# Input projection of a hybrid encoder step: seven products per pair of column tiles for two of three token blocks, with partial sums in scratch

## Chip, cores and metric

The kernel runs on one core of one Trainium2 chip. The metric is device time in microseconds (us) of one execution, the median of the runs shown. One profiled execution gives the trace; its times are counted from the first instruction.

## Reference

One layer of a streaming encoder, for 1024 prompt tokens and 8 x 16 sample tokens, D = 2048, all in float32:

```python
xn = rms_norm(x, norm_g)
u, g_pool, c_q, c_kv, k_r, g_mla = split(xn @ w_in)      # 2048 -> 1024, 1024, 512, 256, 64, 1024
pool_out = multiscale_pool(u) * silu(g_pool)             # windows 2, 4, 8, 16; mean minus token; per-group map
q = rms_norm(c_q) @ w_uq;  ckv = rms_norm(c_kv);  kr = rope(rms_norm(k_r))
attn = block-causal attention over ckv (8 heads) ... ;  mla_out = attn * silu(g_mla)
h = x + concat(pool_out, mla_out) @ w_out
y = h + sigmoid(rms_norm(h) @ w_ple_gate + b) * (p @ w_ple)
```

The change is in the first two lines: the norm, the input projection `xn @ w_in` and, in small part, the pooling.

## The kernel before

**Arithmetic.** A float32 value is held as a high and a low part, both of type float32r. `K.split` (L63) makes them: the high part by a copy on ScalarE (ACT, L68, or L71 with a factor), the low part by a subtraction on VectorE (DVE, L69 or L72). A product (`mm3`, L74) takes three matmuls on TensorE (PE): high x high (L77), low x high (L78), high x low (L79). Each has its own weight load (PEld).

**Tiling.** The 1152 tokens are three blocks of 384 columns (prompt, prompt, 256 prompt plus 128 sample tokens). The contraction of 2048 is 16 row tiles of 128. The input projection has 30 column tiles of 128 plus the rope key of 64 columns, which is held as a high and a low half in one 128-column tile.

**Phase 1** (`phase1`, L131) does the whole input projection. It splits all of x^T times the norm's gain once, into `A0`, `A1`, `A2` (L184, loads L180). It never normalises x: a block's row factors `R` (one over the root mean square) multiply what leaves PSUM. They come from a second reading of x in natural layout, `xnat` (`row_factor`, L191: loads on ACT's queue L196, squares with an accumulator L197, a reciprocal root, a broadcast through three transposes, `spread` L93). Then, for each column tile, `load_w` (L104) brings 4 pieces of weights `wraw` (128x512) over SyncE's queue (SP, L110), splits them into a ring of five `wh`/`wl`, and for each block `project` (L123) runs 16 products, 48 matmuls, into one PSUM bank `mm`:

```python
for i, (kind, ct) in enumerate(cts[9:]):                         # L284, the later column tiles
    w, wn = wn, weights(...)                                     # weights one column tile ahead
    for t in range(NT):
        if kind == "gp":
            gated(pp, kind, ct - 8, t, w)                        # project, times R, SiLU, to scratch
            continue
        ps = mm_bank()
        project(k, ps[:, :TB], w, xh[t], xl[t])
        if late:
            pool.mix(*late)
```

The order of column tiles is: latents and rope key, query latents, pooling gates `gp`, pooling input `u`, attention gates `gm`. The pooling class `Pool` (L375) reads `u` straight from PSUM (L422), forms the window sums by doubling on GpSimd (POOL, L402), the mean minus token on DVE (L406), splits it, and maps it (`mix`, L439: 12 matmuls per output tile, gate L455).

**Hand-over.** Phase 2's first tiles (`load_kv` L561, `latent` L541, keys L597) lie where block 0's `A0` lay, so its loads start when block 0's last product is done, while blocks 1 and 2 of the last column tile still run (`left.close()`, L311).

**Order.** The order of the instructions on each engine is laid down when the kernel is built, by a scheduler that simulates a timeline (`schedule_with_timeline_sim=True`) and prefers what stands earlier in the program. On the chip each engine then runs its list in that order.

Of the kernel before, what the change touches and what calls it, by code (L numbers as in the profile page):

```python
# [14 lines left out]
D = 2048  # L15
# [23 lines left out]
class K:  # L39
    """Shared handles: the context, constants and small helpers."""  # L40
# [22 lines left out]
    def split(self, hi, lo, src, scale=None, eng=None):  # L63
        """src (times a per-partition scale) as hi + lo, each of float32r's width."""
        nc = self.nc
        eng = eng or nc.vector
        if scale is None:
            nc.scalar.activation(hi, src, AF.Copy)  # L68
            eng.tensor_tensor(lo, src, hi, ALU.subtract)  # L69
        else:  # L70
            nc.scalar.activation(hi, src, AF.Copy, scale=scale)  # L71
            eng.scalar_tensor_tensor(lo, src, scale, hi, ALU.mult, ALU.subtract)  # L72
# [8 lines left out]
    def rsqrt(self, pool, y, v, tag):  # L81
        """y = v ** -0.5 for v > 0, by Newton steps from an exponent-halving seed."""
# [10 lines left out]
    def spread(self, pool, ps, out, r):  # L93
        """out[:, j * P + q] = r[q, j] on every partition."""
# [9 lines left out]
def load_w(k, wp, src, chunks=range(KT // WKC), scales=None, bufs=5):  # L104
    """Row chunks of a column tile of a weight [128, KT, 128], as hi and lo tiles of WKC row tiles."""
# [17 lines left out]
def project(k, ps, w, xh, xl, kts=range(KT)):  # L123
    """psum[128, TB] = w^T x over the row tiles kts, of which x holds just these."""
# [5 lines left out]

def phase1(k, sc):  # L131
# [5 lines left out]
    es, left = ExitStack(), ExitStack()  # L137
    # the first block's input leaves before the others'
    ap = [left.enter_context(tc.tile_pool(name="p1a", bufs=1, reuse_waits="tile")),
          es.enter_context(tc.tile_pool(name="p1b", bufs=1, side="right", reuse_waits="tile"))]  # L140
    wp = es.enter_context(tc.tile_pool(name="p1w", bufs=1, side="right", reuse_waits="tile"))
    rp = es.enter_context(tc.tile_pool(name="p1r", bufs=1, side="right", reuse_waits="tile"))
    mp = es.enter_context(tc.tile_pool(name="p1m", bufs=1, space=PSUM, reuse_waits="tile"))
    xh, xl = zip(*[[k.t(ap[t > 0], [P, KT, TB], f"A{t}{x}", F32R) for x in "hl"] for t in range(NT)])
    R = [k.t(rp, [P, TB], f"R{t}") for t in range(NT)]

    def mm_bank():
        return k.t(mp, [P, 512], "mm", bufs=4)

    def aux_bank():  # L150
        return k.t(mp, [P, 512], "aux", bufs=2)

    # order of the column tiles: latents and rope key first, gates of B last
    cts = [("ckv", 20), ("ckv", 21), ("kr", 0)] + [("cq", 16 + i) for i in range(4)]
    cts += [("gp", 8 + i) for i in range(8)] + [("u", i) for i in range(8)]

    def weights(kind, ct):
        if kind != "kr":
            return load_w(k, wp, io["w_in"][ct])
        out = []  # L160
        for c in range(KT // WKC):
            raw = k.t(wp, [P, WKC, DR], "wraw", bufs=3)
            nc.sync.dma_start(raw[:], io["w_kr"][:, c * WKC:(c + 1) * WKC, :])
            hl = k.t(wp, [P, WKC, P], "wh", F32R, bufs=5)
            k.split(hl[:, :, :DR], hl[:, :, DR:], raw[:])
            out.append(hl)
        return out
# [6 lines left out]
    w0 = {}  # L174
    with tc.tile_pool(name="p1x", bufs=1, side="right", reuse_waits="tile") as xp:
        for t in range(NT):
            # the very first pieces are short
            for a, b in ([(0, 1), (1, 2)] if t == 0 else [(0, 2)]) + [(j, j + 2) for j in range(2, KT, 2)]:
                raw = k.t(xp, [P, 2, TB], "xraw", bufs=8)
                nc.sync.dma_start(raw[:, :b - a, :], io["xT"][t][:, a:b, :])  # L180
                if t == 0 and a % WKC == 0:
                    w0.update(load_w(k, wp, io["w_in"][cts[0][1]], [a // WKC]))
                if t == 0 and a == 0:
                    consts(k)  # L184
                for i in range(a, b):
                    k.split(xh[t][:, i, :], xl[t][:, i, :], raw[:, i - a, :], k.norm_g[:, i:i + 1])

    nc.sync.dma_start(k.ident[:], io["ident"])
    stats = [(k.t(rp, [P, 3, 4], f"part{t}"), k.t(rp, [P, 3], f"ssq{t}"), k.t(rp, [P, 3], f"inv{t}")) for t in range(NT)]

    def row_factor(xp, t, j):  # L191
        """Sums of squares of token tile j of block t; after the last one the block's row factors, in steps."""
        part, v, r = stats[t]
        for i in range(4):
            raw = k.t(xp, [P, D // 4], "xnat", bufs=3)
            nc.scalar.dma_start(raw[:], io["xN"][3 * t + j][:, i * D // 4:(i + 1) * D // 4])  # L196
            nc.scalar.activation(raw[:], raw[:], AF.Square, accum_out=part[:, j, i:i + 1])  # L197
        if j == 2:
            nc.vector.tensor_reduce(v[:], part[:], AX.X, ALU.add)
            nc.vector.tensor_scalar(v[:], v[:], 1.0 / D, EPS, ALU.mult, ALU.add)  # L200
            k.rsqrt(xp, r[:], v[:], "rs")
            yield
            yield
            yield
            k.spread(xp, aux_bank(), R[t], r)

    def latent_factor(lp, kind, t, acc):
        """The row factors of a block's latents, from the lanes' sums of squares."""
        yield
        yield  # L210
        a = aux_bank()
        for j in range(3):
            nc.tensor.matmul(a[:, j:j + 1], acc[:, j * P:(j + 1) * P], k.ones[:, :1], start=True, stop=True)
        r = stats[t][2]
        v = k.t(lp, [P, 3], "lv")
        s = k.t(lp, [P, 3], "ls")
        nc.vector.tensor_tensor(v[:], r[:], r[:], ALU.mult)
        nc.vector.scalar_tensor_tensor(v[:], a[:, :3], 1.0 / (KVR if kind == "ckv" else QR), v[:], ALU.mult, ALU.mult)
        nc.vector.tensor_scalar_add(v[:], v[:], EPS)
        k.rsqrt(lp, s[:], v[:], "lrs")  # L220
        nc.vector.tensor_tensor(s[:], s[:], r[:], ALU.mult)
        yield
        yield
        out = k.t(lp, [P, TB], "srow")
        k.spread(lp, aux_bank(), out, s)
        nc.sync.dma_start(sc["s_" + kind][t][:], out[:])

    def gated(pool, kind, n, t, w):
        ps = mm_bank()
        project(k, ps[:, :TB], w, xh[t], xl[t])  # L230
        k.tick()
        ev = k.t(pool, [P, TB], "ev", bufs=3)
        nc.vector.tensor_tensor(ev[:], ps[:, :TB], R[t][:], ALU.mult)  # L233
        nc.scalar.activation(ev[:], ev[:], AF.Silu)
        nc.sync.dma_start(sc[kind][t][:, n, :], ev[:])

    # latents: raw projections and their row factors, normalised where they are read back
    with tc.tile_pool(name="p1c", bufs=1, side="right", reuse_waits="tile") as lp:
        kc = k.t(lp, [P, 9, DR], "kc")
        ks = k.t(lp, [P, 9, DR], "ks")  # L240
        rope_tables(k, lp, kc, ks, io["k_rope_g2"], 1.0)
        acc = {}
        for i, (kind, ct) in enumerate(cts[:7]):
            w, wn = (w0 if i == 0 else wn), weights(*cts[i + 1])
            for t in range(NT):
                ps = mm_bank()
                if kind == "kr":
                    for kt in range(KT):
                        st = w[kt // WKC][:, kt % WKC, :]
                        nc.tensor.matmul(ps[:, :TB], st, xh[t][:, kt, :], start=kt == 0, stop=False)  # L250
                        nc.tensor.matmul(ps[:, :TB], st, xl[t][:, kt, :], start=False, stop=kt == KT - 1)
                    k.tick()
                    k.later(rope_key(k, lp, aux_bank, ps, R[t], kc, ks, t, sc))
                    continue
# [25 lines left out]
    with tc.tile_pool(name="p1p", bufs=1, side="right", reuse_waits="tile") as pp:  # L280
# [20 lines left out]
        for t in range(NT):  # L301
            gated(pp, "gm", 0, t, w)
            if t == 0:
                pool.mix(*late)
# [1076 lines left out]
```

## Time and profile before

| | |
|---|---|
| runs (us) | 2322.14, 2326.36, 2325.97; median 2325.97 |
| span of the profiled execution | 2321.7 us; its own time is not listed apart, the nearest run is 0.4 us above the span, the median 4.3 us |
| phase 1 on PE | first matmul at 5.9 us, last of block 2 at 826.7 us |
| PE busy over the span | 2263.2 us (97%) |
| DVE, ACT, POOL busy | 1153.4, 844.8, 382.3 us |
| mean granted TensorE clock | 0.990 |

Busy PE is not PE at its peak: the records of neighbouring matmuls overlap (a 128x384 matmul is recorded with some 335 ns, and one starts every 173 ns or so). Work on PE is therefore read from counts and starts, and idle PE from the waits. What an engine other than PE does costs time only where PE ends up waiting for it.

### The profile page before, as it was taken

Reading aid. Unit: us, or ns where it says so; the run is one execution under the profiler, and the core shown is the slowest. Engines: PE = TensorE matmul, PEld = TensorE weight load, DVE = VectorE, ACT = ScalarE, POOL = GpSimd, SP = SyncE. Lnnn points to the kernel's source line nnn. Section 1 sums busy time; section 2 is a strip of 40 time slices with the busy share of each in tenths; the row PEclk is TensorE's granted clock in tenths of the full one; section 3 lists DMA queues with packets and bytes.
Section 4 is the critical chain, followed back from the end, with each engine's and each line's share of the span. In section 5 each row is a group of like instructions: output and inputs, shape, how many; then the busy total and the mean of one; then the engine's idle time right before and its main releaser. Section 6 shows DMA issues by size and latency. Waiting matters only on the chain.

```text
span 2321.7 us, 35417 instructions
## 1 busy us (share of the span) xinstructions
PE 2263.2 (97%) x13198; PEld 2207.8 (95%) x13198; DVE 1153.4 (50%) x2636; ACT 844.8 (36%) x1967; POOL 382.3 (16%) x357
## 2 busy tenths in 40 slices
PE   8899999999999999989999799999999999999999
PEld 8899999999999989978898699999999999999998
DVE  6443111334312169868988865555553335344343
ACT  6421111111111166766665453434342234222222
POOL 0000000123300000014443342212002221111110
PEclk9999999999999999999999899999999999999999
DMA  7522212333312186573221663434263334223221
GB/s 279 171 98 69 74 65 82 70 88 92 81 61 75 47 244 185 152 221 104 83 68 54 217 204 126 152 128 150 88 190 100 110 106 130 85 86 101 85 86 63
DMA packets 219661, 271.05 MB, mean 117 GB/s; under 512 B 38112, under 2 KB 160480, under 8 KB 219488
## 3 DMA queue, kind: packets, MB, share of 16 engines
q1 hardware_dynamic: 199616, 242.43, 33.4%
q10 hardware_dynamic: 19872, 26.35, 3.4%
q8 instruction: 104, 1.70, 0.3%
q14 instruction: 69, 0.57, 0.1%
HBM read 196.10 MB, written 72.61 MB: 116 GB/s over the span
## 4 chain that ended last, share of the span: by engine, by line
PE 80%; DVE 8%; DMA 7%; issue 2%; ACT 1%; POOL 1%; SPq 0%; ACTq 0%; DVEq 0%; POOLq 0%
PE mm L79 18%; PE mm L77 18%; PE mm L78 18%; PE f L77 3%; PE f L79 3%; PE f L78 3%; DMA xnat<-xN 2%; PE k L78 2%; PE k L77 2%; PE k L79 2%; PE t L919 1%; PE pb L77 1%; PE pb L79 1%; PE o L79 1%; PE pb L78 1%
## 5 line engine op out<-in xcount | busy, mean ns | idle before, releaser
L77 PE MATMUL mm<-A0h,wh 128*128 128x384 f32 x736 | 250.3, 340 | 6.7 <-ACT A0h L71 5.9
L78 PE MATMUL mm<-A0h,wl 128*128 128x384 f32 x736 | 249.7, 339 | 1.0 <-DVE wl L69 1.0
L79 PE MATMUL mm<-A0l,wh 128*128 128x384 f32 x736 | 249.8, 339 | 0.0
L77 PE MATMUL mm<-A1h,wh 128*128 128x384 f32 x736 | 246.6, 335 | 0.2 <-ACT ev L263 0.2
L79 PE MATMUL mm<-A2l,wh 128*128 128x384 f32 x736 | 246.6, 335 | 0.0
L77 PE MATMUL mm<-A2h,wh 128*128 128x384 f32 x736 | 246.5, 335 | 0.0
L78 PE MATMUL mm<-A2h,wl 128*128 128x384 f32 x736 | 246.4, 335 | 0.0
L79 PE MATMUL mm<-A1l,wh 128*128 128x384 f32 x736 | 246.3, 335 | 0.1
L78 PE MATMUL mm<-A1h,wl 128*128 128x384 f32 x736 | 246.3, 335 | 0.0
L69 DVE TENSOR_TENSOR wl<-wraw,wh 128x512 fp32r<-128x512 f32 (+1 forms) x232 | 157.4, 679 | 153.4 <-ACT wh L68 147.7
L68 ACT ACTIVATE wh<-wraw 128x512 fp32r<-128x512 f32 (+1 forms) x236 | 137.4, 584 | 246.8 <-PE mm L79 193.6
L77 PEld LDWEIGHTS mm<-A0h,wh 128*128 128x128 f32 x736 | 139.3, 189 | 7.4 <-ACT A0h L71 5.9
L78 PEld LDWEIGHTS mm<-A0h,wl 128*128 128x128 f32 x736 | 139.2, 189 | 1.8 <-DVE wl L69 1.8
L79 PEld LDWEIGHTS mm<-A0l,wh 128*128 128x128 f32 x736 | 139.1, 189 | 0.2 <-DVE A0l L72 0.2
L79 PEld LDWEIGHTS mm<-A1l,wh 128*128 128x128 f32 x736 | 138.2, 188 | 1.0 <-DVE A1l L72 0.7
L77 PEld LDWEIGHTS mm<-A1h,wh 128*128 128x128 f32 x736 | 138.2, 188 | 0.8 <-ACT ev L263 0.5
L77 PEld LDWEIGHTS mm<-A2h,wh 128*128 128x128 f32 x736 | 138.2, 188 | 0.0
L79 PEld LDWEIGHTS mm<-A2l,wh 128*128 128x128 f32 x736 | 138.2, 188 | 0.0
L78 PEld LDWEIGHTS mm<-A2h,wl 128*128 128x128 f32 x736 | 138.2, 188 | 0.0
L78 PEld LDWEIGHTS mm<-A1h,wl 128*128 128x128 f32 x736 | 138.2, 188 | 0.0
L233 DVE TENSOR_TENSOR ev<-mm,R 128x384 f32<-128x384 f32 x48 | 26.8, 558 | 224.3 <-PE mm L79 224.3
L1239 DVE TENSOR_TENSOR ev<-mm,R 128x384 f32<-128x384 f32 x48 | 26.8, 557 | 174.1 <-PE mm L79 170.2
(437 smaller groups left out, 5511.6 us busy)
## 6 DMA issues: line engine op xcount, KB each, us to landing
wraw<-w_in SPq DMA_DIRECT2D x120, 256.0 KB, 3.1
wraw<-w_out SPq DMA_DIRECT2D x64, 256.0 KB, 3.6
wraw<-w_ple_gate SPq DMA_DIRECT2D x64, 256.0 KB, 3.3
xnat<-xN ACTq DMA_DIRECT2D x36, 256.0 KB, 3.5
ple<-ev ACTq DMA_DIRECT2D x48, 192.0 KB, 2.5
fev<-xT SPq DMA_DIRECT2D x48, 192.0 KB, 2.4
hp<-fev SPq DMA_DIRECT2D x48, 192.0 KB, 1.9
ev<-hp SPq DMA_DIRECT2D x48, 192.0 KB, 2.3
```

The source lines that it names most:

```text
L68: nc.scalar.activation(hi, src, AF.Copy)
L69: eng.tensor_tensor(lo, src, hi, ALU.subtract)
L77: mm(out, sh, mh, start=start, stop=False)
L78: mm(out, sl, mh, start=False, stop=False)
L79: self.last = mm(out, sh, ml, start=False, stop=stop)
L233: nc.vector.tensor_tensor(ev[:], ps[:, :TB], R[t][:], ALU.mult)
L919: nc.tensor.transpose(tp[:, x, :], e[:, (c + x) * P:(c + x + 1) * P], k.ident[:])
L1239: nc.vector.tensor_tensor(g[:], ps[:, :TB], R[t][:], ALU.mult)
```

## The change

For blocks 0 and 1, the two token blocks together with the two halves of a contraction chunk make a 2 x 2 block matrix, and a pair of column tiles with the same halves make another. Their product is formed by Strassen's scheme in Winograd's form: seven products instead of eight, from sums of the input blocks (`S1` to `S4`) and sums of the weight tiles. Because the sums need normalised inputs, x of blocks 0 and 1 is normalised before it is split. The contraction is cut into two chunks of 8 row tiles. The order becomes:

1. *Front.* Chunk 0 of block 2 alone, plain, for the first 26 column tiles (24 matmuls each), while x of blocks 0 and 1 is loaded, its squares are summed, and the operands of chunk 0 are formed.
2. *Chunk 0*, 15 pairs: seven products of 4 row tiles (84 matmuls), block 2 only in the last two pairs. Results go to scratch (`part1`). Meanwhile the operands of chunk 1 are formed and put in scratch (`sums`) in pairs 5, 7, 9 and 11.
3. *Switch.* The 28 operands of chunk 1 come back from scratch and are split; block 2's next 8 row tiles too.
4. *Chunk 1*, 15 pairs: 84 matmuls plus 48 for block 2. The chunk-0 sums are read back and either copied into a PSUM bank before the product (by ACT) or added after it (by DVE). The pooling now reads `u` back from scratch, and its window sums move from GpSimd to DVE.
5. *Hand-over.* Phase 2's loads start after the last pair; block 2 of the last two column tiles (48 matmuls) follows.

The `xnat` loads are gone. Weights are split in pieces of 8 row tiles (128x1024), again in a ring of five; the raw pieces have three buffers. The last two products of a pair (`tail`) are issued after the next pair's first two. The rope key keeps its four products per chunk. Core of the diff:

```diff
+    def sums(self, src, c, rest):                       # weights of a pair, one pair ahead
+        r0, r1 = [self.raw(s, c) for s in src]
+        w0 = self.hl(r0)
+        a = k.t(self.tp, [P, 8, P], "wt")
+        sub(a[:, :4], r1[:, :4], r0[:, :4], ALU.subtract)
+        sub(a[:, 4:], r1[:, 4:], a[:, :4], ALU.subtract)
+        w12 = self.hl(a)
+        sub(r0[:, :4], r1[:, 4:], r1[:, :4], ALU.subtract)
+        sub(r0[:, 4:], r0[:, 4:], a[:, 4:], ALU.subtract)
+        w34 = self.hl(r0)
+        w1 = self.hl(r1, 0 if rest else 4)
+        return {1: (w0, 0), 2: (w0, 4), 5: (w12, 0), 6: (w12, 4), 7: (w34, 0), 4: (w34, 4), 3: (w1, 4),
+                "rest": ((w0, 0), (w1, 0))}
...
+    def pair(self, c0, c1, A, X, W, prior, done, between):
+        def bank(*i):
+            ps = self.bank()[:, :TB]
+            if prior and i:
+                nc.scalar.activation(ps, prior(*i)[:], AF.Copy)
+            return ps
...
+        a, b = bank(), bank(c0, 1)
+        q = prior and prior(c0, 0)
+        self.product(a, x("11"), W[1], True)
+        s1 = tile("s1", 2)
+        nc.scalar.activation(s1[:], a, AF.Copy)
+        d = bank(c1, 1)
+        self.product(b, x("S2"), W[6], start)
+        u2 = tile("u2", 2)
+        add(u2[:], b, s1[:], ALU.add)
+        self.tail()                                     # W[4], W[3] of the pair before
+        between(0)
+        e = [X and bank(c0, 2)]
+        self.product(a, x("12"), W[2], False)
+        done(c0, 0, a, q)
+        self.product(d, x("S1"), W[5], start)
+        between(1)
+        e.append(X and bank(c1, 2))
+        self.product(b, x("S3"), W[7], False)
+        u3 = tile("u3")
+        add(u3[:], b, s1[:], ALU.add)
...                                                     # with X: both tiles of block 2, 24 matmuls each
+    steps += [lambda c=c: row(c) for c in range(16)] + [norms, normalise]
+    steps += [lambda j=j: first_operands(j) for j in range(4)]
+    for i in range(EARLY):                              # front; EARLY = 26
+        w, wn = wn, qk.hl(qk.raw(src[i + 1], 0)) if i + 1 < EARLY else None
+        e = bank()[:, :TB]
+        qk.product(e, X, (w, 0), True, 8)
+        step(2)
+        keep(i, 2, e, None)
...
+    def row(c):                                         # one row tile of blocks 0 and 1: 768 columns
+        for t in range(2):
+            nc.scalar.dma_start(raw[:, t * TB:(t + 1) * TB], io["xT"][t][:, c, :])
+        squares(R, raw[:], ...)                         # ACT square, DVE add
+    def operands(j, a11, a12, a21, a22, s, put):        # 7 splits, 4 subtractions
...
+    for n in OPS:                                       # switch: "11", "S2", "12", "S1", "S3", "22", "S4"
+        for j in range(4):
+            raw = k.t(ap, [P, TB], f"a{j}")
+            nc.sync.dma_start(raw[:], sc["sums"][:, 4 * OPS.index(n) + j, :])
+            put(n, j, raw[:])
...
-            nc.gpsimd.tensor_tensor(nxt[..., a:L], cur[..., a:L], cur[..., a - step:L - step], ALU.add)
+            nc.vector.tensor_tensor(nxt[..., a:L], cur[..., a:L], cur[..., a - step:L - step], ALU.add)
...
-        nc.vector.tensor_tensor(u[:, HIST:], ps[:, :n], R[:, :n], ALU.mult)
+        nc.sync.dma_start(u[:, HIST:], src[t][:, ct, :])
...
+    left.close()                                        # after the last pair's tail
+    yield
+    for i in range(2):                                  # block 2 of the last two column tiles
+        e = bank()[:, :TB]
+        nc.scalar.activation(e, prior(2 * last + i, 2)[:], AF.Copy)
+        qk.product(e, X, W["rest"][i], False, 8)
```

More of the change, by code (lines that the diff above doesn't have):

```diff
@@ L157, in weights @@
[L157 to L167, printed above, removed]
+    xp = es.enter_context(tc.tile_pool(name="p1x", bufs=1, side="right", reuse_waits="tile"))
@@ L171, in phase1 @@
     nc.scalar.activation(k.ones[:], k.ones[:], AF.Copy)
[L174 to L186, printed above, removed]
@@ L188, in phase1 @@
-    nc.sync.dma_start(k.ident[:], io["ident"])
[L189 to L205, printed above, removed]
@@ new lines, in last_block, with squares @@
+    def last_block(c, j):
+        i = 8 * c + j
+        raw = (o_tile() if c else k.t(rp, [P, 2 * TB], f"x{j}"))[:, :TB]
+        nc.sync.dma_start(raw, io["xT"][2][:, i, :])
+        hl = [k.t(xp, [P, TB], f"X{j}{x}", F32R) for x in "hl"]
+        k.split(hl[0][:], hl[1][:], raw, k.norm_g[:, i:i + 1])
+        if c == 0:
+            squares(R2, raw, raw)
+        return hl
+    begun = set()
+    def squares(acc, raw, sq):
+        if id(acc) not in begun:
+            begun.add(id(acc))
+            nc.scalar.activation(acc[:], raw, AF.Square)
+        else:
+            nc.scalar.activation(sq, raw, AF.Square)
+            nc.vector.tensor_tensor(acc[:], acc[:], sq, ALU.add)
@@ new lines, in factors @@
+    def factors(pool, acc, n, dim, wait=1):
+        a = aux_bank()
+        for j in range(n):
+            nc.tensor.matmul(a[:, j:j + 1], acc[:, j * P:(j + 1) * P], k.ones[:, :1], start=True, stop=True)
+        v = k.t(pool, [P, n], f"fv{n}")
+        r = k.t(pool, [P, n], f"fr{n}")
+        nc.vector.tensor_scalar(v[:], a[:, :n], 1.0 / dim, EPS, ALU.mult, ALU.add)
+        k.rsqrt(pool, r[:], v[:], f"frs{n}")
+        for _ in range(wait):
+            yield
+        for j in range(0, n, 3):
+            k.spread(pool, aux_bank(), acc[:, j * P:(j + 3) * P], r[:, j:j + 3])
@@ new lines, in phase1, with chunk, weights @@
+    OPS = ("11", "S2", "12", "S1", "S3", "22", "S4")
+    pairs = range(KR // 2)
+    def chunk(c, prior, done, between, pairs=pairs):
+        def weights(m):
+            return qk.sums(src[2 * m:2 * m + 2], c, c or 2 * m >= EARLY)
+        W = weights(pairs[0])
+        for m in pairs:
+            if m == 2:
+                key(c, prior, done)
+            Wn = weights(m + 1) if m + 1 in pairs else None
+            qk.pair(2 * m, 2 * m + 1, A, X if c or 2 * m >= EARLY else None, W, prior, done, lambda i: between(m, i))
+            W = Wn
@@ new lines, in prepare @@
+    def prepare(m, i):
+        if i == 1 and m in (5, 7, 9, 11):
+            second_operands((m - 5) // 2)
+        if i == 1 and m < 4:
+            square_rest(8 + 2 * m)
+            square_rest(9 + 2 * m)
+        if i == 1 and m == 4:
+            k.later(factors(ep, R2, 3, D))
+        if i == 0:
+            k.tick()
+    chunk(0, None, keep, prepare)
+    qk.tail()
+    for n in OPS:
[3 more added lines that the diff above has]
+            put(n, j, raw[:])
@@ new lines, in phase1, with mixer @@
+    pool = Pool(k, mp, aux_bank, inv, sc, wp)
+    def mixer(m, i):
+        if 8 <= m < 12 and i == 0:
+            g = m - 8
+            for t in range(NT):
+                steps.extend([lambda c=c, t=t: pool.tile(2 * g + c, t) for c in range(2)])
+                if t:
+                    steps.append(lambda t=t: pool.mix(g, t - 1))
+                else:
+                    steps.append(lambda: pool.weights(g))
+                steps.append(pool.split)
+            steps.append(lambda: pool.mix(g, NT - 1))
+        step(2)
@@ L313, in phase1 @@
+    chunk(1, prior, finish, mixer, range(6, KR // 2 - 1))
+    last = KR // 2 - 1
+    W = qk.sums(src[2 * last:], 1, True)
+    qk.pair(2 * last, 2 * last + 1, A, None, W, prior, finish, lambda i: mixer(last, i))
+    qk.tail()
+    left.close()
+    yield
+    for i in range(2):
+        e = bank()[:, :TB]
+        nc.scalar.activation(e, prior(2 * last + i, 2)[:], AF.Copy)
+        qk.product(e, X, W["rest"][i], False, 8)
+        finish(2 * last + i, 2, e, None)
+        step(len(steps))
     es.close()
```

388 lines of the change are left out of this document (252 added, 136 removed).

## Prediction

> **What bounds the kernel now.** I read the page's head first, then the busy time by stages, the groups of matmuls, and the waits of PE up to the end of phase 1. Columns of a stage: its length, then busy time of PE, PEld, DVE, ACT and POOL with counts, granted clock, DMA share, GB/s. A wait row ends with total, times, longest.
>
> ```profile
> span 2321.7 us, 35417 instructions
> PE 2263.2 (97%) x13198; PEld 2207.8 (95%) x13198; DVE 1153.4 (50%) x2636; ACT 844.8 (36%) x1967; POOL 382.3 (16%) x357
> ...
> 6.00:100.00 94.00, 84.57 (x448) 80.42 (x449) 50.04 (x122) 59.92 (x141) 0.00 (x0) 0.96 0.75 259
> 100.00:826.00 726.00, 726.00 (x4190) 725.65 (x4189) 208.13 (x463) 124.06 (x216) 66.18 (x104) 1.00 0.26 78
> ...
> 200.00:400.00 200.00, 200.00 (x1157) 199.89 (x1156) 41.33 (x92) 34.42 (x59) 0.11 (x1) 1.00 0.21 69
> ...
> L77 PE MATMUL mm<-A0h,wh x480: 335/338/688, 5.9 to 809.7; 128*128 128x384 f32 x160
> L79 PE MATMUL mm<-A2l,wh x480: 334/334/421, 30.8 to 826.7; 128*128 128x384 f32 x160
> ...
> PE mm L77 <- ACT A0h L71: 5.9, 1, 5.9
> PE aux L100 <- DVE sq L98: 4.5, 2, 2.4
> PE aux L213 <- ACT R L101: 2.9, 1, 2.9
> ```
>
> PE bounds it. From 100 to 826 us it never idles; one matmul starts every 200 / 1157 = 0.173 us at full clock, with DVE busy 29% and ACT 17%. The only losses of phase 1 stand in its first 100 us: the start, and the chain of the row factors. So each matmul taken out of phase 1 is worth 0.173 us, as long as DVE, ACT and the queues, which have room, stay ahead.
>
> **The matmuls.** Before: 30 column tiles x 3 blocks x 48 = 4320, plus 96 for the rope key. After: front 26 x 24 = 624; two chunks x 15 pairs x 7 products x 12 = 2520; block 2 in the pairs, 4 x 24 + 30 x 24 = 816; rope key again 96. Together 4056, which is 360 fewer: **-62.3 us**. The mixer's 144 matmuls and the transposes stay. Everything else in the change can only take from this, except the front.
>
> Prices (mean ns in the grouped rows; the rows that begin with a time have start and us):
>
> ```profile
> L69 DVE TENSOR_TENSOR wl<-wraw,wh 128x512 fp32r<-128x512 f32 x26 | 18.0, 693 | 34.5 <-ACT wh L68 34.4
> L69 DVE TENSOR_TENSOR wql<-raw,wqh 128x768 fp32r<-128x768 f32 x8 | 7.6, 953 | 1.6 <-ACT wqh L68 1.6
> 816.12 1.23 DVE L69 TENSOR_TENSOR wkl<-raw,wkh 128x1024 fp32r<-128x1024 f32 x1
> L233 DVE TENSOR_TENSOR ev<-mm,R 128x384 f32<-128x384 f32 x19 | 10.6, 558 | 100.5 <-PE mm L79 100.5
> L69 DVE TENSOR_TENSOR dl<-d,dh 128x384 fp32r<-128x384 f32 x24 | 13.8, 573 | 11.3 <-ACT dh L68 11.3
> L72 DVE SCALAR_TENSOR_TENSOR A0l<-xraw,gains,A0h 128x384 fp32r<-128x384 f32 x16 | 8.9, 617 | 0.8 <-ACT A0h L71 0.8
> L455 DVE SCALAR_TENSOR_TENSOR ev<-aux,gains,ev 128x384 f32<-128x384 f32 x24 | 14.4, 611 | 5.9 <-PE aux L79 4.4 <-DMA ev<-gp 1.5
> L406 DVE SCALAR_TENSOR_TENSOR d<-s,u 128x384 f32<-128x384 f32 x16 | 8.9, 555 | 13.5 <-POOL s L402 13.5
> L68 ACT ACTIVATE ch<-raw 128x1024 fp32r<-128x1024 f32 x16 | 16.9, 1055 | 18.4 <-PE k L79 11.7 <-DMA raw<-cache_T 6.7
> L263 ACT ACTIVATE ev<-mm 128x384 f32<-128x384 f32 x18 | 8.4, 487 | 36.4 <-PE mm L79 36.4
> ev<-gp SPq DMA_DIRECT2D x24, 192.0 KB, 2.4
> ```
>
> **Chunk 0, 15 pairs of 84 matmuls, 14.5 us each.** DVE has 4 subtractions (4 x 0.69), splits of 3.5 pieces (3 x 1.23 + 0.69) and 7 operations on 384 columns (7 x 0.56): 11.1 us. ACT has 3.7 splits and copies, about 5 us. In pairs 5, 7, 9 and 11 the operands of chunk 1 add 4 x 0.62 + 4 x 0.56 = 4.7 us, so 15.8 of 14.5. The ring of five allows this delay: the slot of the next pair's first weights comes free after `W[3]` of the pair before, that of its second after `W[2]`; each is wanted three products (6.2 us) later, and copy plus subtraction take 1.06 + 1.23. So 3.9 us of lateness on DVE is free in each pair. How PE fares beside a full DVE is seen in later stages of this kernel:
>
> ```profile
> 850.00:900.00 50.00, 49.72 (x291) 47.52 (x290) 42.20 (x132) 37.24 (x138) 0.00 (x0) 0.98 0.59 178
> 1100.00:1150.00 50.00, 48.31 (x295) 45.53 (x294) 44.56 (x87) 32.31 (x64) 21.87 (x15) 1.00 0.21 69
> 1200.00:1250.00 50.00, 46.72 (x289) 43.83 (x288) 45.38 (x87) 31.03 (x62) 22.96 (x14) 1.00 0.15 54
> 1250.00:1300.00 50.00, 44.47 (x240) 39.38 (x238) 43.57 (x99) 24.74 (x52) 16.78 (x12) 0.93 0.35 107
> 1300.00:1350.00 50.00, 41.83 (x227) 37.27 (x228) 40.77 (x78) 29.40 (x69) 24.74 (x21) 0.86 0.79 251
> ```
>
> With DVE at 84% PE loses 0.6%, with DVE at 91% 6.6%. On the 243 us of chunk 0 that is 1 to 16 us; DVE averages (15 x 11.1 + 4 x 4.7 + 5) / 243 = 78% there, nearer the first: **+2**.
>
> **Chunk 1, 15 pairs of 132 matmuls, 22.8 us.** DVE: 2.8 + 4 x 1.23 + 9 x 0.56 = 12.7 us; room enough in pairs 0 to 7. From pair 8 the pooling comes on top, all on DVE now: window sums by L406's price, 20 doublings x (3 x 0.555 or so, the third block in two pieces), 35; the means 14; splits 24 x 0.573 = 14; gates 24 x 0.611 = 15: some 80 us. Pairs 8 to 14 take PE 7 x 22.8 + 144 x 0.173 = 185 us, DVE 7 x 12.7 + 80 = 169, or 91%. By the two rows above 1 to 12 us: **+5**. The seeding of PSUM (4 per pair) waits for a load and an ACT copy, 2.4 + 0.49; six banks let it start two products (4.1 us) ahead, so I cost it at nothing; without this cover it is 2.9 us per pair, 44 in all. SP issues some 14 transfers per pair. A weight load behind one that waits for DVE waits too; that is in the 5.
>
> **Switch.** 28 operands and 8 tiles of block 2 (192 KB each) and 1 MB of weights, 8 MB, against the 27 us of pair 14: 300 GB/s; DVE 28 x 0.573 + 8 x 0.62 + 7.7 = 29 us in the same time. Operands leave in the order in which PE last uses them, so most of it can run under pair 14. The nearest row is 1300 to 1350, a change of stage at 251 GB/s: PE idle 8.2 us, and 0.14 of the clock besides (7 us). Bounds 0 and 15, **+5**.
>
> **Front.** The first matmul still waits for one split each of x and weights (5.9). Then per column tile (24 matmuls, 4.15 us) 512 KB of weights come in and 192 KB go out; the row tiles add 6 MB: 27 MB in 114 us, 233 GB/s, less than the 259 that the first 100 us carry now. DMA volume is no new bound, but the engines are tight:
>
> ```profile
> 0.00:25.00 25.00, 17.22 (x81) 15.03 (x82) 18.12 (x34) 19.64 (x36) 0.20 (x4) 1.00 0.92 335
> ...
> ACT xnat L197 <- DMA xnat<-xN: 26.9, 22, 4.5
> ...
> 48.29 0.33 ACTq L196 DMA_DIRECT2D xnat<-xN  x1
> ...
> 93.27 0.83 PE L213 MATMUL aux<-ones,acc 128*128 128x1 f32 x6 [2.87 <-ACT R L101]
> ...
> 95.00:96.70 1.70, 1.70 (x7) 1.70 (x6) 1.43 (x9) 0.18 (x1) 0.00 (x0) 0.50 0.96 340
> ```
>
> ACT stood 26.9 us waiting for 36 loads of x. The new loop has 16 row tiles of the same kind: 26.9 x 16 / 36 = 12 us of such waits. Beside them ACT has, per column tile, 1.06 + 2 squares of 768 columns (0.85 each, between the rows of 384 and 1024) + 0.49 + the issue of four loads (0.33 each): 4.6 against 4.15 us, 4 us over 8 column tiles. After the last of them DVE has a block of work that ranks before later weights: normalising 8 x 0.95, operands 28 x 0.573 + 16 x 0.56, 33 us. The five slots feed PE for 5 x 4.15 = 21 us, so up to 12 us are lost. Upper bound 12 + 4 + 12 = +28. The gain side: the waits for the row factors (4.5 + 2.9) and the slow clock after them go away, since nothing needs them until the operands: -10. In between, **+8**.
>
> [...]
>
> **Hand-over.** Rows of before:
>
> ```profile
> 810.10 0.34 PE L79 MATMUL mm<-A0l,wh 128*128 128x384 f32 x1
> 810.47 0.56 SPq L538 DMA_DIRECT2D raw<-w_kv  x1
> 826.30 1.23 DVE L69 TENSOR_TENSOR wvl<-raw,wvh 128x1024 fp32r<-128x1024 f32 x1 [1.45 <-ACT wvh L68]
> ```
>
> Phase 2's first four weight pieces take 17 us from the release, and 96 matmuls (16.6 us) covered that. Now 48 matmuls (8.3 us) stand there, so up to 8.7 us show. But the released memory is 28 separate operands, of which several end one to six products before the tail; **+2**.
>
> **Sum.** -62.3 + 2 + 5 + 5 + 8 + 2 = -40 us. The profiled span of 2321.7 becomes 2281.5; it lies 4.3 us under the median 2325.97, so the forecast against the median is **2286 us**.
>
> **Rivals.**
> - *Everything is hidden*: only the matmuls count, 2326 - 62 = 2264, down to 2254 with the front's gain. For it: phase 1 shows no PE wait after 100 us. Against: DVE doubles its load there.
> - *The front starves*: +28 instead of +8, 2306. For it the 26.9 us row.
> - *Slower: the weight ring in both chunks.* If the low part of the next weights stands behind a whole set of sums and one output (7.2 + 1.1 us) in DVE's list, a chunk-0 pair lasts 4.4 us more, 15 x 4.4 = 66: 2352. It decides against the change from 2.7 us per pair, a lateness of 6.6. For it: the sums of the next pair stand ahead of this pair's outputs in the program; against: the row 850 to 900.
> - *The clock oscillates.* Three banks are cycled every 12 matmuls instead of one every 48; short waits at each change could bring the 0.93 of the row 1250 to 1300 over all of phase 1's 730 us: 2286 + 51 = 2337. No wait at a change of bank shows between 100 and 826 us. [...]
> - *No gain*: matmuls in the new order start 0.010 us later each (40 / 4056), 2326. No row speaks for it.
>
> **Chances.** Forecast 0.53 (own range 2270 to 2302), all hidden 0.15, front 0.12, ring 0.13, clock 0.04, no gain 0.03. Low end between the hidden case's two values, 2256; high end 2330, which leaves out ring and clock above and little below. What a measurement can tell is about 0.2% (4.6 us): faster 0.79, same 0.04, slower 0.17.
>
> **What would show it.** 4056 `mm` matmuls in phase 1 at 0.173 us; its last about 40 us earlier; PE waits for DVE low parts in the front after some 50 us, few in chunk 0; DVE near 75% in chunk 0, 90% in the pooling pairs; a dip of PE and 250 GB/s or more near 360 to 390 us. The forecast falls if PE waits for `w` low parts in every pair, or if the front runs past 140 us.

## Result and the profile after

The changed kernel took 2343.03 us (median; 2336.01 to 2347.59) where the kernel before took 2326.16: ratio 1.0070, 95% interval 1.0052 to 1.0088. Timed again later beside three of its variants it took 2332.44 us against 2323.72, ratio 1.0036 (1.0023 to 1.0048); a single execution in between took 2322.7. It is slower, by 0.4 to 0.7% in the two sittings (sets of runs timed together) with more than one execution, where 1.7% faster was forecast.

Two profiles are used: the first (2347.59 us, span 2345.8), the longest of its four executions, and that of the second timing (2327.80 us, span 2326.0), the shortest of its five. Head of the page of the first:

```profile
span 2345.8 us, 35907 instructions
PE 2232.0 (95%) x12856; PEld 2168.6 (92%) x12856; DVE 1472.4 (63%) x3096; ACT 975.2 (42%) x2117; POOL 316.4 (13%) x261
```

PE is busy 31 us less than before and idle 55 us more. Where, the windows show; I cut them at front, chunk 0, pairs 0 to 7 of chunk 1, pairs 8 to 14 (the pooling), hand-over (to phase 2's first key product), rest. Columns as in the prediction. The first profile, then the second:

```profile
0.00:129.00 129.00, 117.12 (x643) 113.84 (x644) 91.94 (x135) 76.07 (x122) 0.20 (x4) 0.97 0.70 228
129.00:386.80 257.80, 251.11 (x1415) 250.43 (x1414) 187.47 (x295) 88.30 (x129) 0.00 (x0) 0.98 0.53 166
386.80:590.70 203.90, 199.38 (x1154) 197.80 (x1153) 139.70 (x310) 86.44 (x147) 0.22 (x2) 0.99 0.55 170
590.70:829.70 239.00, 206.39 (x1093) 203.26 (x1091) 152.38 (x298) 63.82 (x108) 0.67 (x6) 0.91 0.61 159
829.70:1043.20 213.50, 190.56 (x1050) 171.42 (x1049) 164.37 (x500) 139.52 (x467) 1.94 (x8) 0.98 0.62 188
1043.20:2345.80 1302.60, 1267.41 (x7509) 1231.81 (x7509) 736.58 (x1559) 521.07 (x1145) 313.37 (x241) 0.98 0.37 117
```
```profile
0.00:127.20 127.20, 116.93 (x642) 113.96 (x643) 91.80 (x135) 76.56 (x122) 0.20 (x4) 0.97 0.69 231
127.20:383.60 256.40, 249.95 (x1415) 249.27 (x1414) 188.31 (x296) 89.73 (x131) 0.00 (x0) 0.99 0.52 168
383.60:586.90 203.30, 199.29 (x1155) 197.89 (x1154) 138.10 (x309) 85.16 (x145) 0.22 (x2) 0.99 0.53 168
586.90:816.30 229.40, 201.34 (x1093) 197.53 (x1091) 153.03 (x299) 64.23 (x109) 0.67 (x6) 0.95 0.62 166
816.30:1029.40 213.10, 192.89 (x1051) 174.13 (x1049) 164.27 (x501) 140.07 (x467) 1.95 (x8) 0.96 0.62 190
1029.40:2326.00 1296.60, 1263.53 (x7509) 1227.78 (x7509) 735.12 (x1559) 521.09 (x1145) 313.27 (x241) 0.99 0.36 117
```

The same cuts of the kernel before: its first 100 us and its end from the last projection product:

```profile
0.00:100.00 100.00, 84.65 (x448) 80.50 (x449) 50.81 (x123) 62.78 (x145) 0.20 (x4) 0.97 0.74 256
826.70:1025.60 198.90, 188.40 (x1052) 173.32 (x1050) 158.81 (x492) 135.61 (x461) 2.28 (x8) 0.97 0.62 186
1025.60:2321.70 1296.10, 1263.47 (x7509) 1227.62 (x7509) 735.21 (x1559) 522.04 (x1145) 313.68 (x241) 0.99 0.37 117
```

Length less count times 0.173 is what a stage loses (counts of a window may miss or gain a few records; I use the program's: 642, 1413, 1152 and 1091 with the mixer's products and transposes):

| term | forecast | first profile | second |
|---|---|---|---|
| 360 matmuls fewer | -62.3 | -62.3 | -62.3 |
| front, against 22.4 lost before | +8 | -4 | -6 |
| chunk 0 | +2 | +13 | +12 |
| switch and pairs 0 to 7 | +5 | +5 | +4 |
| pairs 8 to 14 with the pooling | +5 | +50 | +41 |
| hand-over, against 198.9 | +2 | +15 | +14 |
| rest, against 1296.1 | 0 | +7 | +1 |
| sum | -40 | +24 | +4 |

The spans differ from before by +24.1 and +4.3. One term carries most of the error, 45 of the 64 us in the first profile: the pooling pairs. Of their 50 us some 33 are idle time of PE (239.0 less 206.4), and nearly all the rest is the granted clock of 0.91 in that row (206.4 x 0.09 = 19 us, an estimate). There, in the first profile (waits of PE, DVE and SP's queue in 590 to 830 us; total, times, longest):

```profile
PE aux L77 <- DVE ev L726: 25.5, 6, 11.0
PE aux L77 <- ACT dh L68: 5.5, 2, 5.0
```
```profile
DVE s L675 <- DMA u<-u: 32.7, 16, 6.3
DVE ev L726 <- DMA ev<-gp: 22.2, 13, 5.3
```
```profile
SPq L721 <- DMA mixp<-ev: 29.4, 17, 6.3
SPq L727 <- DVE ev L726: 21.4, 14, 4.8
```

PE waits 25.5 us for the gated product (`ev`, L726), because its two auxiliary banks are both still unread. DVE is not full there (152.4 of 239 us, 64%): it stands waiting for what comes back from scratch, `u` (L675) and the gate (L726). And SP's queue, which issues nearly everything, waits 29.4 us to issue the next gate load (L721) until the store of the last product from the same single buffer has landed. A stretch of 31 us from the chain of waits of that profile, start and us, has it in line:

```profile
736.57 5.64 DMA mixp<-ev
742.23 4.25 DMA ev<-gp
746.58 0.62 DVE ev L726
747.22 1.85 DMA mixp<-ev
749.09 2.53 DMA ev<-gp
751.85 0.44 issue
752.39 5.09 DMA mixp<-ev
757.55 2.63 DMA ev<-gp
760.20 0.63 DVE ev L726
760.84 1.88 DMA mixp<-ev
762.78 4.53 DMA ev<-gp
```

Store, load, 0.6 us of work, store, load: in this stretch PE and ACT are off the chain, and DVE is on it for 0.6 us at a time. Later in the stage (768 to 802 us) the chain also holds runs of DVE's own operations, beside loads of `u`.

### The profile page after: what moved, and what is told of

Same layout as the page of the kernel before. It is cut to its first block, busy times and chain, and to the rows that moved or that the text cites. A ratio compares the mean times of both kernels' runs of the same rounds, so it can differ in the third digit from the quotient of the medians.

```text
span 2345.8 us, 35907 instructions
## 1 busy us (share of the span) xinstructions
PE 2232.0 (95%) x12856; PEld 2168.6 (92%) x12856; DVE 1472.4 (63%) x3096; ACT 975.2 (42%) x2117; POOL 316.4 (13%) x261
## 4 chain that ended last, share of the span: by engine, by line
PE 50%; DVE 8%; DMA 8%; issue 2%; ACT 1%; POOL 0%; SPq 0%; ACTq 0%; DVEq 0%; POOLq 0%
PE mm L77 8%; PE mm L79 8%; PE mm L78 8%; PE f L77 3%; PE f L79 3%; PE f L78 3%; PE k L79 2%; PE k L78 2%; PE k L77 2%; PE t L1190 1%; DMA ev<-gp 1%; PE pb L77 1%; PE s L78 1%; PE s L77 1%; PE pb L79 1%
## 5 line engine op out<-in xcount | busy, mean ns | idle before, releaser
L68 ACT ACTIVATE wh<-wraw 128x1024 fp32r<-128x1024 f32 (+3 forms) x233 | 178.7, 769 | 233.3 <-PE mm L177 141.9
L69 DVE TENSOR_TENSOR wl<-wraw,wh 128x1024 fp32r<-128x1024 f32 (+3 forms) x231 | 205.8, 892 | 64.8 <-ACT wh L68 61.8
L1511 ACT ACTIVATE ev<-ev,gains 128x384 f32<-128x384 f32 x48 | 29.4, 612 | 224.5 <-DVE ev L1510 124.4
L77 PE MATMUL k<-wkh,ch 128*128 128x448 f32 x256 | 96.3, 377 | 2.5 <-ACT ch L68 1.4
L1318 DVE TENSOR_REDUCE v<-sq 128x8 f32<-128x1024 f32 x64 | 77.7, 1213 | 14.5 <-ACT sq L1317 14.2
L79 PE MATMUL mm<-A2l,wh 128*128 128x384 f32 x256 | 86.1, 336 | 0.0
L77 PE MATMUL mm<-A2h,wh 128*128 128x384 f32 x256 | 86.0, 336 | 0.0
L77 PE MATMUL mm<-A0h,wh 128*128 128x384 f32 x256 | 85.8, 335 | 0.0
L79 PE MATMUL mm<-A0l,wh 128*128 128x384 f32 x256 | 85.7, 335 | 0.0
L78 PE MATMUL mm<-A1h,wl 128*128 128x384 f32 x256 | 85.7, 335 | 0.0
L78 PE MATMUL mm<-A0h,wl 128*128 128x384 f32 x256 | 85.7, 335 | 0.0
L79 PE MATMUL mm<-A1l,wh 128*128 128x384 f32 x256 | 85.5, 334 | 0.0
L77 PE MATMUL mm<-A1h,wh 128*128 128x384 f32 x256 | 85.5, 334 | 0.0
```

Source lines behind the costliest of these rows:

```text
L77: mm(out, sh, mh, start=start, stop=False)
L78: mm(out, sl, mh, start=False, stop=False)
L79: self.last = mm(out, sh, ml, start=False, stop=stop)
L1318: nc.vector.tensor_reduce(v[:, j, :], sq[:].rearrange("p (h d) -> p h d", h=H), AX.X, ALU.add)
L1511: nc.scalar.activation(g[:], g[:], AF.Sigmoid, bias=k.b_ple_gate[:, ct:ct + 1])
```

## Experiments

All ratios are to the kernel before, timed beside it, with 95% intervals.

**First set: one suspect each.** Two gate buffers; two input buffers; window sums back on GpSimd; no gate.

```diff
-            gate = k.t(pp, [P, TB], "ev")                     # e1_gate2
+            gate = k.t(pp, [P, TB], "ev", bufs=2)
-        u = k.t(pp, [P, HIST + TB], "u")                      # e6_u2
+        u = k.t(pp, [P, HIST + TB], "u", bufs=2)
-            nc.vector.tensor_tensor(nxt[..., a:L], ...)       # e2_gpsimd
+            nc.gpsimd.tensor_tensor(nxt[..., a:L], ...)
-            nc.sync.dma_start(gate[:], sc["gp"][t][:, n, :])  # e4_nogate; the product is scaled per channel only
```

> The changed kernel with two buffers instead of one for the mixer's gate tile. Theory A (the gate's one buffer makes store, next load and scaling a chain of some 5 us per output, DVE stands in line for the load, PE for the PSUM bank): PE's waits for the scaling from 615 to 826 us fall from 25.5 us to under 10, most of the half-clock time after them goes too, 20 to 35 us faster than the changed kernel's median of 2343. Theory B (DVE is simply full in the pooling pairs, because the window sums moved to it): within 5 us of 2343, and the waits stay.

> The changed kernel with two buffers instead of one for the pooling input tile that is read back from scratch. Theory A in its narrow form (the gate's buffer alone): within 5 us of 2343. Theory A in its wide form (every load from scratch into a single buffer stands in DVE's line; DVE idled 33 us before the first window sum): DVE's idle time before the window sums falls from 33 to under 15 us and the time by 8 to 20 us. Theory B: within 5 us.

> The changed kernel with the window sums back on GpSimd, all else as changed. Theory A: no gain, within 8 us of 2343 to either side, since a sum lasts 0.85 us on GpSimd against 0.57 on DVE and the chain gets longer. Theory B (DVE's load): DVE loses some 35 us of work between 615 and 826 us, PE's waits there halve, 15 to 25 us faster.

> The changed kernel with the mixer's gate left out: the mapped output is scaled by the per-channel scale alone and stored, and the gate is never loaded. Theory A: the load is gone from the chain, only the store of 2 us stands between two scalings; the waits for the scaling nearly vanish and it is 25 to 40 us faster than 2343, a little more than with two buffers. Theory B: at most 5 us, since DVE's work is the same.

| | time (us) | ratio | pairs 8 to 14 (us) |
|---|---|---|---|
| two gate buffers | 2324.51 | 0.9998 (0.9984 to 1.0012) | 220.1 |
| two input buffers | 2333.2 | 1.0035 (1.0022 to 1.0047) | 223.2 |
| sums on GpSimd | 2338.74 | 1.0072 (1.0052 to 1.0091) | 233.5 |
| no gate | 2326.7 | 1.0008 (0.9998 to 1.0018) | 216.6 |

Taking the window sums off DVE gained nothing, though not on equal terms, since DVE then waited 22.7 us for GpSimd's sums. It points away from DVE's amount of work as the bound; the run without loads, below, decides it. The other three shorten the stage. Without the gate PE still waited 12.9 us for the scaled product, and 16 us were gained in the reading below where 25 to 40 were expected: the gate's load is not the whole loss. I read 18.5 and 10 us of gain for the buffers against the first timing of the changed kernel, made in another sitting; that reading did not hold (below).

**Second set: the edits together, and the other two terms.** Both buffers; the second half's operands held on DVE to the pairs they were written for; the last two block-2 tiles held behind the tail; all four.

```diff
+        k.mark = add(u2[:], b, s1[:], ALU.add).ins            # e8_held
-            second_operands((m - 5) // 2)
+            with tc.issue_after(k.mark):
+                second_operands((m - 5) // 2)
     qk.tail()
+    held = k.last.ins                                         # e3_tailfirst
...
+        with tc.issue_after(held):
+            qk.product(e, X, W["rest"][i], False, 8)
```

> Gate tile and pooling input tile both with two buffers (the small window tile of the last tile of each channel borrows a slot of the output ring to make room). Theory A (single buffers chain the loads, each its own chain): the gains add, 2343 - 18.5 - 10 = 2314; 2311 to 2319, last product of phase 1 at 800 to 805 us, PE's waits for the gate product and DVE's waits for the pooling input both under 10 us between 590 and 830. Rival (one chain, and either buffer already breaks it): no more than the better of the two, 2322 to 2326, last product near 809.

> Only the second half's operands are held on DVE behind the pair they are written for (pairs 5, 7, 9 and 11 of the first chunk). Theory C (the loss of chunk 0 is these operands, issued at 135 to 185 us with the key's weights and the squares): PE's window 150 to 175 goes from 18.3 to over 23 us at a clock over 0.9, chunk 0 shortens by 8 to 12 us, time 2331 to 2336. Rival D (chunk 0 has no room for the operands anywhere; a later pair loses what this one gains): chunk 0 stays within 3 us, time 2340 to 2345.

> Only the two block-2 tiles held back for the hand-over are issued behind the last pair's tail, so all 48 of their matmuls cover it instead of 24. Theory E (the cover of the hand-over was half spent early): PE's waits from 826 to 900 us fall from 13.8 to 8 to 10, last product of phase 1 to first key product from 213.5 to 208 to 210, time 2337 to 2341. Rival F (the fill in the pooling stage was worth as much as the cover, or the waits are loads that 4 us of cover do not reach): time 2342 to 2346.

> All four edits: two buffers for gate and pooling input, second operands held to their pairs, block-2 tiles behind the tail. If the three losses are separate, the sum is 2343 - 28 - 10 - 4 = 2301, and 2296 to 2308, faster than the kernel before by about 1 per cent. If they share one cause (DVE's total work, so that what one place gains another gives back) it stays at 2316 to 2326, no faster than the kernel before or hardly.

| | time (us) | ratio | chunk 0 | pairs 8 to 14 | hand-over |
|---|---|---|---|---|---|
| both buffers | 2320.69 | 0.9993 (0.9981 to 1.0004) | 256.4 | 222.7 | 209.0 |
| operands held | 2325.0 | 1.0008 (0.9999 to 1.0017) | 251.2 | 229.2 | 213.0 |
| tiles behind tail | 2332.94 | 1.0041 (1.0025 to 1.0056) | 257.0 | 232.5 | 208.7 |
| all four | 2311.41 | 0.9943 (0.9930 to 0.9955) | 251.2 | 221.7 | 210.9 |

The buffers do not add: 222.7 us with both, 220.1 and 223.2 with one. That is the rival's number, but one chain is not shown by it: to make room, this edit also puts the pooling's small state tile into the ring of the outputs, and DVE waits there for an output store (`gm<-o`, 7.4 us) as with neither single edit. All four together, 2311.4 us, lie between the two forecasts (2296 to 2308 if the losses are separate, 2316 to 2326 if they are one). What still waits with both buffers is seen in the all-four profile's waits of SP's queue in 590 to 826 us: the same line, now L725, still 32.4 us.

```profile
SPq L725 <- DMA mixp<-ev: 32.4, 11, 4.6
SPq L532 <- ACT o L531: 18.5, 9, 7.9
```

The cause in chunk 0 is shown in size only for part of it: the window 150 to 175 of the changed kernel, then of the one with held operands, and DVE's operations on those operands in 130 to 190 us of the first (12 of 16 normalisations, written for pairs 5 to 11, 219 to 322 us):

```profile
150.00:175.00 25.00, 18.31 (x78) 17.67 (x77) 20.07 (x36) 6.07 (x9) 0.00 (x0) 0.80 0.91 291
```
```profile
150.00:175.00 25.00, 22.63 (x128) 21.88 (x127) 14.75 (x23) 8.67 (x13) 0.00 (x0) 1.00 0.46 157
```
```profile
L463 DVE SCALAR_TENSOR_TENSOR a<-a,gains,R 128x384 f32<-128x384 f32 x12 | 7.3, 610 | 1.3 <-DMA a<-xT 1.2
```

Holding them brings 5 to 7 of the 12 to 13 us back (8 to 12 were expected).

**The pooling's own queue, and the changed kernel once more.** All transfers of the pooling (input, state, gate, stores) from GpSimd's queue, alone and with the four edits.

```diff
-        nc.sync.dma_start(u[:, HIST:], src[t][:, ct, :])      # and the six others of tile() and mix()
+        nc.gpsimd.dma_start(u[:, HIST:], src[t][:, ct, :])
```

> The changed kernel with the pooling's own transfers (its input, its state, its gate, its stores) issued from GpSimd's queue, which is idle here, instead of SyncE's; buffers as they were. Theory Q (one in-order queue: each pooling load or store that waits holds back the weights, prior sums and output stores behind it, and is held back by them): pairs 8 to 14, 229 to 239 us now, fall to 205 to 220, PE's waits for the gate product and SP's waits in that stage under half, time 2318 to 2332. Rival V (it is volume: 174 GB/s and 0.7 of the DMA engines there, where the kernel before moved 69 GB/s, so each transfer lands late whichever queue issues it): pairs 8 to 14 stay at 225 to 240, time 2336 to 2346, or longer, since GpSimd's transfers must be prepared by GpSimd.

> All four earlier edits and the pooling's transfers on GpSimd's queue. Theory Q: pairs 8 to 14, 221 us with the four edits, come near the 200 us that their products and the mixer's take, last product of phase 1 at 785 to 795, time 2294 to 2304. Rival V: within 4 us of 2311, last product at 800 to 806.

> The changed kernel once more, unaltered, to see how far its stages repeat from profile to profile. If pairs 8 to 14 take 239 us again (235 to 242), the 229 us of the build with the held operands is that build's order of instructions; if they come out at 228 to 234, 10 us of that stage are scatter and no difference of that size between builds may be read there.

Alone: 2323.82 us, ratio 0.9995 (0.9985 to 1.0004), pairs 8 to 14 in 214.6 us. With the four edits: **2291.49 us, ratio 0.9857 (0.9843 to 0.9872)**, pairs 8 to 14 in 199.1 us, last product at 782.0, faster than both kernels. Its window of that stage moves about the same bytes as the changed kernel's in less time (39 MB at 196 GB/s, where the changed kernel has 38 MB at 159), so volume is not the bound:

```profile
582.90:782.00 199.10, 193.33 (x1094) 191.93 (x1093) 152.59 (x301) 65.45 (x109) 64.26 (x114) 0.98 0.72 196
```

The unaltered kernel took 2322.7 us in its one execution there, with 226.4 us for the pooling pairs: the 20 us between the timings were not the edits'. Beside that one execution the queue alone (2323.82 us) shows no gain in time. So three edits were timed again beside the changed kernel.

**On one chip, side by side.**

> The changed kernel, unaltered, timed beside the others of this call. If the first figure holds everywhere: 2336 to 2347, ratio to the kernel before 1.005 to 1.009. If it hangs on the chip or on the execution: 2320 to 2335, with a spread of over 10 us, ratio 0.998 to 1.004. Pairs 8 to 14 take between 225 and 240 us either way, against the 185 to 190 of their products.

> Two buffers for the gate tile, timed beside the changed kernel. If the single gate buffer costs what was read between two chips: 15 to 20 us under the changed kernel of this call. If the difference was the chip's: within 5 us of it.

> The pooling's transfers on GpSimd's queue, beside the changed kernel. Theory Q (one in-order queue): 10 to 20 us under it, pairs 8 to 14 at 210 to 218 us against 225 to 240. If volume: within 5 us of it.

> The second half's operands held to their pairs, beside the changed kernel. Chunk 0 is shorter by 6 to 7 us in the profile (251.5 against 257 to 258); if nothing else comes of it the time is 5 to 8 us under the changed kernel's; the 18 us read between two chips would be the chip's for the rest.

| | time (us) | ratio | against the changed kernel | pairs 8 to 14 |
|---|---|---|---|---|
| changed kernel | 2332.44 | 1.0036 (1.0023 to 1.0048) | | 229.4 |
| two gate buffers | 2321.93 | 0.9987 (0.9978 to 0.9996) | -10.5 | 221.5 |
| pooling's own queue | 2321.21 | 0.9989 (0.9979 to 0.9999) | -11.2 | 214.3 |
| operands held | 2327.57 | 1.0015 (1.0005 to 1.0024) | -4.9 | 230.3 |

Each gains, between a quarter and three fifths of what I had read between sittings. Two input buffers and tiles behind the tail, at 1.0035 and 1.0041 in their sittings, are not told from the changed kernel's 1.0036. The queue alone takes 15 us out of the stage as it is cut here, and 11 off the time. Part of the 15 is only moved: in both its profiles the last 9 of the pooling's 144 map products come behind the last projection product, and the last scaling starts at 827 and 834 us where the changed kernel of this sitting has it at 814. From the start of pair 8 it is, in the profile of this sitting, 231.2 us to the first product of phase 2, against 234.5, and 428.9 us to the first key product, against 442.5. PE's wait for the gated product (590 to 826 us) fell from 22.8 to 18.7 us only, where under half was expected: with its one buffer DVE now waited 35.3 us for the gate's load instead of 21.4. In both profiles, too, the stage from first key product to first score is 309 us instead of 299 to 304, for which I have no cause.

**What is left.** The pooling without its loads (input zeroed once, gate left out, two buffers for the product; all sums, splits, products and stores kept); block 2 of the last two pairs held behind the tail, which loads the weights of the earlier pair a second time; the stores of the silu outputs from ACT's queue. The last two start from the version with five edits.

```diff
-        nc.sync.dma_start(u[:, HIST:], src[t][:, ct, :])      # e13_noload; u is one zeroed tile, no gate load, "ev" with bufs=2
-    chunk(1, prior, finish, mixer, range(6, KR // 2 - 1))     # e12_cover; pair 13 without block 2, done after the tail
+    chunk(1, prior, finish, mixer, range(6, KR // 2 - 2))
-        nc.sync.dma_start(sc[kind][t][:, n, :], o[:])         # e14_actstore, for gp and gm
+            nc.scalar.dma_start(sc[kind][t][:, n, :], o[:])
```

> The changed kernel without the pooling's loads: its input tile is zeroed once and read by every window, the gate is left out and the output is scaled per channel alone (two buffers); every sum, split, product and store of the pooling stays. If the loads' latency is the whole loss of the stage, pairs 8 to 14 fall from 229 to 190 to 200 us and the time to 2292 to 2305. If DVE's work or the stores make up part of it, they stay over 208 us and the time over 2312.

> The version with all five edits, and block 2 of the last two pairs, 96 matmuls or 16.6 us, instead of the last one, 48, held behind the last pair's tail, with the weights of the earlier pair loaded once more. If the hand-over's loss is cover, the span from the last tail product to the first key product, less the held products, falls by 5 to 9 us and the time to 2283 to 2288. If it is the volume of loads at that point, which the reloaded weights add to, the time stays at 2289 to 2296.

> The version with all five edits, and the stores of the silu outputs issued from ACT's queue, behind the silu that makes them, instead of SyncE's. If SyncE's waits for these outputs (50 us in pairs 8 to 14) hold back weights and prior sums: DVE's wait for the weights there falls from 9 us to under 4 and the time to 2282 to 2288. If nothing that is late stands behind them: 2289 to 2296.

Without loads: 2294.91 us, ratio 0.9884 (0.9864 to 0.9903); pairs 8 to 14 take 191.0 us against 188.7 of products. Its stage, and the same stage of the changed kernel in the second profile:

```profile
615.00:650.00 35.00, 35.00 (x201) 35.00 (x201) 26.74 (x54) 10.72 (x18) 0.00 (x0) 1.00 0.57 145
650.00:700.00 50.00, 50.00 (x287) 50.00 (x286) 41.80 (x81) 18.24 (x29) 0.00 (x0) 1.00 0.62 171
700.00:750.00 50.00, 50.00 (x289) 50.00 (x288) 45.94 (x92) 21.58 (x39) 0.00 (x0) 1.00 0.63 150
```
```profile
615.00:650.00 35.00, 25.62 (x138) 25.33 (x137) 21.20 (x45) 8.59 (x15) 0.22 (x2) 0.85 0.67 163
650.00:700.00 50.00, 45.10 (x242) 44.59 (x241) 32.03 (x63) 10.67 (x18) 0.22 (x2) 0.93 0.69 180
700.00:750.00 50.00, 43.79 (x236) 42.09 (x234) 37.05 (x72) 18.00 (x31) 0.11 (x1) 0.97 0.67 175
```

With DVE at 84 and 92% (41.80 and 45.94 of 50), PE does not idle at all. So DVE's work is not the bound, and the loads, with the single buffer of the gate that went with them, are nearly the whole loss of the stage: 38 of 41 us.

Doubled cover: 2304.34 us, ratio 0.9917 (0.9900 to 0.9933), above both forecasts and 13 us above the version it started from, which was timed in another sitting. From last tail product to first key product it takes 228.3 us, less 16.6 held: 211.7; the version with five edits 218.9 less 8.3: 210.6. That does not show that cover is of no use: the held products fill 24.2 us, not 16.6, because a map product of the pooling stands before the last two of them and PE waits 4.7 us there (`PE aux L77 <- ACT dh L68`). From the last projection product to the first key product it is 204.1 us against 210.6, so the longer cover did shorten what follows it, and the version lost elsewhere (the part behind the first key product is 1307.3 us against 1299.6). Stores on ACT's queue: 2296.09 us, 0.9887 (0.9868 to 0.9905), no gain, again across sittings: DVE's wait for weights in that stage fell from 9.0 to 4.3 us, but 5.0 us of waiting for a prior sum stood in its place.

## Why the prediction was wrong

*The step that failed* is the pooling's +5, which measured +41 to +50. I counted DVE's work, 80 us on top of seven pairs, got 91%, and took two bounds from how PE fares beside a busy DVE. The work was sized rightly enough (152 us of busy time where I had 169), but it did not set the pace. A third row of the same view of the kernel before, beside the two that I used, has DVE at 91% and PE idle for 0.3 us only:

```profile
900.00:950.00 50.00, 49.71 (x290) 45.75 (x289) 45.60 (x143) 35.04 (x112) 2.28 (x8) 1.00 0.70 206
```

What the change did to the pooling is this: `u`, which had been read from PSUM into one of two buffers, now goes to scratch and back into a single one, and the gate and its product, which went through scratch before too, share one buffer instead of three. Each is a transfer of 2.2 to 3 us (medians in the two profiles), on one queue with weights, prior sums and outputs. I had the price in hand (`ev<-gp`, 2.4 us) and used it for the seeds of PSUM only; of "a weight load behind one that waits" I said that it was in the 5. Multiplied out, 24 gate tiles with a store and a load of 2.4 us each on one buffer make 115 us of chain, and 24 input tiles at the same 2.4 us another 58: 173 us in a stage of 185, before anything else stands in the queue. This is an estimate that adds the two chains as if they never ran side by side; it gives no loss by itself, but it says that they had to be priced. No share of DVE tells that.

How the queue and the buffers divide it: two gate buffers take 8 us out of the stage, the queue 15 (partly moved, as said), all five edits 27 to 30, no loads 38, the last two read across sittings. For the queue the cleaner pair is the four edits without and with it, 221.7 and 199.1 us: every map product lies inside the stage in both. The transfers themselves became slower on GpSimd's queue (medians from issue to landing in 590 to 800 us of the second profile, then in 587 to 800 with the queue alone):

```profile
mixp<-ev SPq DMA_DIRECT2D x21, 192.0 KB, 2.2
ev<-gp SPq DMA_DIRECT2D x21, 192.0 KB, 2.4
```
```profile
mixp<-ev POOLq DMA_DIRECT2D x21, 192.0 KB, 2.8
ev<-gp POOLq DMA_DIRECT2D x21, 192.0 KB, 3.5
```

So it is the standing in line that was saved, not the transfer. Choosing the queue by these medians alone would have been wrong here. The queue also takes time of GpSimd: the version with five edits has it busy 382.6 us in 373 instructions over its whole span, the changed kernel (first profile) 316.4 us in 261. That is 112 more, as many as the pooling has transfers, and 66 us / 112 = 0.6 us each; in pairs 8 to 14 it is 64.26 us (114), where the changed kernel has 0.67 (6). Where the map products stand in PE's order may matter too: no run changed that order alone, so how much of the loss a later place would have hidden is open.

*Hand-over*, +2, measured +14 to +15. That 48 matmuls cover less than 96 was right, but the bound of 8.7 us did not hold: the released memory did not come early (phase 2's first load was issued at 825.5 us, 4 us before the last product), and the order of PE has 20 of the 48 ahead of the tail, in the pooling's gaps. With all 48 behind the tail the four builds that have it show 208.7 to 210.9 us, the one with 96 shows 204.1, the changed kernel and the builds that leave this order 209.0 to 215.7, the kernel before 198.9: more cover seems to help by a few us, and does not close it. The first 45 us of phase 2, before and after:

```profile
827.00:850.00 23.00, 19.58 (x79) 16.44 (x78) 13.96 (x37) 13.97 (x39) 0.00 (x0) 0.83 0.93 286
850.00:875.00 25.00, 24.78 (x141) 23.96 (x140) 19.18 (x58) 20.38 (x75) 0.00 (x0) 0.95 0.71 211
```
```profile
830.00:850.00 20.00, 11.41 (x40) 8.17 (x40) 10.27 (x21) 10.75 (x32) 0.00 (x0) 0.83 0.90 287
850.00:875.00 25.00, 20.68 (x99) 17.09 (x98) 21.69 (x64) 16.97 (x53) 0.00 (x0) 0.93 0.97 302
```

PE idles 13 us here where it idled 4, with the DMA engines at 0.9 or more. That the loads of phase 2 come all at once fits; it was only argued. Open.

*Chunk 0*, +2, measured +12 to +13. The average of 78% was near (73%, 187.5 of 257.8), but the work was not spread as I put it: the scheduler issued most of the second half's operands some 60 us and more early, beside the key's weights. PE idles 6.7 us there (257.8 less 251.1), in two waits of 3.6 and 3.1 us; most of the rest is the granted clock, 0.98 over the stage and 0.80 from 150 to 175 us. Holding the operands returns 5 to 7; the rest is open. *The front*, +8, was 12 to 14 too pessimistic: ACT waited for its loads of x as priced (11.2 us where I had 12), but no wait of PE names them; it lasts 127 to 129 us. *Switch*, +5: right. *Matmuls*: right, 4056 at 0.173. *Rivals*: the ring did not show (pairs 6 to 12 of chunk 0 start 14.6 us apart where 14.5 were computed, so the 3.9 us of slack held); the clock was low where PE had waited, 0.91 in the pooling stage of the first profile, and 0.98 to 0.99 over chunk 0 and over pairs 0 to 7. (Around PE's longest wait in the pooling stage, 10.96 us up to 645.19 us, the clock reads 0.50 from 638 to 651 us; in the kernel before it reads 0.50 from 95.00 to 96.70 us, after a wait of 2.87 us that ended at 93.27 us.) No rival named the one that came.

With the pooling's waits mostly gone the time comes near the sum: the version with five edits has 2291.5 us, against the forecast of 2286. That is luck in part: its front (127.0 us) is some 14 us better than forecast, which makes up for its chunk 0 (251.4) and hand-over (210.6), together some 15 us worse.

## What to carry to other kernels

Price a value that is sent to memory and back as a chain, not as bytes or busy time: store, load, use, times the tiles, divided by the buffers, and see which queue it stands in and behind what; a stage may fail at 64% of its busiest helper. A busy share says little where the buffers are single. When a change saves memory by cutting rings from three to one, look there first.

The kernel paced by these chains scattered by 20 us from one sitting to the next, where the kernel before stayed within 3; judge an edit beside its parent, in one sitting on one chip.

## What was not expected of the hardware

The unaltered changed kernel took 2343.0, 2322.7 and 2332.4 us in three sittings, while the kernel before took 2326.2, 2323.5 and 2323.7. The scatter lies in the pooling pairs (239.0, 226.4, 229.4 us) and, in the first, in the rest of the kernel (1302.6 against 1296.6); the last two were made on different chips, and whether that is what differs no run shows.

A DVE busy 92% of a window (45.94 of 50 us without the pooling's loads) cost PE nothing, where the 91% that the prediction took from a later stage of the kernel before stood beside 6.6% of idle PE. The share alone does not make the loss; what made it in that later stage no run shows.
